# Order of the second running products, of the context state and of the second outputs in a linear-attention scan on one Trainium2 core

## Chip, cores and metric

One core of a Trainium2 chip. The metric is the device time of one execution in microseconds (us). TensorE is PE in the profile, VectorE is DVE, ScalarE is ACT, GpSimd is POOL and SyncE is SP; PEld is PE's weight load.

## What is computed

A block of a diffusion model on 2048 latent tokens and 256 context tokens, width 1024, in fp32: an adaptively scaled RMS norm, a gated linear recurrence (HGRN2) with 8 heads of 128 by 128 states in both directions, a readout, and a gated feed-forward network with a convolution. The change lies in the recurrence:

```python
def hgrn2_chunk_scan(q, k, v, logf, s0):
    """S_t = diag(f_t) S_{t-1} + k_t v_t^T, o_t = S_t^T q_t, in chunkwise form."""
    ...
    scores = jnp.einsum('bhnik,bhnjk->bhnij', qe, ke)
    scores = jnp.where(mask, scores, 0.0)
    o_intra = jnp.einsum('bhnij,bhnjv->bhniv', scores, v)
    kv = jnp.einsum('bhnjk,bhnjv->bhnkv', k * jnp.exp(b_last - b), v)
    ...
    o_inter = jnp.einsum('bhnik,bhnkv->bhniv', q * jnp.exp(b), s_start)
```

The context tokens are scanned first, from a zero state; their final state in each direction starts the scan of the latent tokens.

## The kernel before

The stage of the change is `mixer_scan`, from about 560 to 1200 us of the span. It runs over two groups of 8 token tiles (g = 0 and 1), and in each group over the 8 heads. A head of group 0 begins with the projections of the context's two gates (`ctx_gates`); each head has two units of four 128-token tiles. For each unit PE projects the two gates (lines 943 to 945, three fp32r matmuls for one fp32 product; forward and backward direction), ACT makes the decay factors of them (967, 969), and then come the unit's steps:

- `factors`: running products of the decay factors on DVE (`tensor_tensor_scan`, 987), the differences "ke" of these (1002, 1003), and small products for each segment on POOL (1009 to 1031), the last of them "sd" (1012).
- `suffix`: the second running products, from the other end (two scans, 1037). They write S over the first ones, so they wait for POOL, which reads these.
- `rest`: the products of queries and keys with those factors (1044, 1045, 1052, 1021).
- `scores`: transposes of the keys (1075, with a copy on ACT, 1077), 96 small score matmuls into "sc" (1119), a masked copy of both directions (`copy_predicated`, 1136) and the sum of the two, "at" (1137).
- `stepped(0)`: the key-value products of the first two tiles into the PSUM tile "kv" (1150), two state updates on DVE (1153), and a copy of the other direction's products on ACT (sk, 1158) that is stored.
- `second`: the outputs of the first two tiles, `outputs(0)` (1173 from the states, 1176 from "at"), and `stepped(1)`.
- `outputs(1)`: the outputs of the last two tiles.

For the context of a head: `keys` (a product on DVE, 1021), a function that transposes them (1075, 1077), and `state`, which multiplies them with the values (1094, into the same PSUM tile "kv"; there is one bank with this tag) and makes the starting states `Sf[h]` and `Sb[h]` of it (1096 on ACT, 1097 to 1100 on DVE).

The order of all this is written as a clock. `at(when, f)` puts a function on an agenda, and each step of a latent projection (three matmuls) advances the clock by one; a step of the context's projection advances it by half. A gate pair of a unit takes 16 steps, that of the context 8. So a head of group 0 takes 40 steps, of group 1 32, and the steps of one unit run among the projections of the next. The numbers in `after` count from the end of the unit's gates. The second unit of a head ends its gates 16 steps after the first, so that the first unit's `scores` (19) come 3 steps after that end, and the second unit's `suffix` (6) 6 steps after it.

The agenda gives only a priority. A planner that works at build time, with costs of its own for each instruction, lays each engine's queue: of the instructions that it expects to be ready it takes the one that was listed first, so one that isn't ready is overtaken. On the chip each engine then runs its queue in that order. `tc.issue_after(i)` adds to this that what is listed in its block stands behind `i` in the queue of `i`'s engine. `tied(f)` uses it: it puts `f` behind the latest state update of a `stepped(0)` (`made_last`).

Of the kernel before, what the change touches and what calls it, by code (L numbers as in the profile page):

```python
# [16 lines left out]
OP = mybir.AluOpType  # L17
# [28 lines left out]
def body(ctx, tc, a, out):  # L46
    nc = tc.nc
    pe, act, dve, pool, sp = nc.tensor, nc.scalar, nc.vector, nc.gpsimd, nc.sync
# [848 lines left out]
    def mixer_scan():  # L897
# [31 lines left out]
        AB = fix.tile([128, 2, UT, 128], F32, name="AB")  # L929
# [140 lines left out]
        def turned(kd, s0, n):  # L1070

            tr = ps.tile([128, n, 2, 128], F32, name="tr", tag="tr")
            for i in range(n):
                for d in range(2):
                    pe.transpose(tr[:, i, d], kd[:, d, 4 * (s0 + i):4 * (s0 + i) + 4], ident)
            kt = gp.tile([128, 2, 2, 128], F32, name="kt", tag="kt", bufs=2)
            act.activation(kt[:, 0:n], tr, AF.Copy)
            return kt
# [31 lines left out]
        def unit_steps(h, t0, m):  # L1110

            kts, states = [], []
            at_ = gp.tile([128, UT, 128], F32, name="at", tag="at", bufs=2)
            q_ = act if h == NH - 1 and t0 == NT - UT else sp

            def scores():

                def score(d, s, k, kc, q, qc):
                    pe.matmul(scs[d][32 * kc:32 * kc + 32, s, 32 * qc.start:32 * qc.stop], k, q,
                              start=True, stop=True, skip_group_check=True)  # L1120

                ke, qp, km = [m[n] for n in ("ke", "qp", "km")]
                kts.append(turned(m["kd"], 0, 2))
                for s in range(UT):
                    for j in range(4):
                        qc = slice(2 - j // 2 * 2, 4 - j // 2 * 2)
                        score(0, s, km[:, s, j], j,
                              qp[:, 1 - j // 2, 4 * s + qc.start:4 * s + qc.stop], qc)
                    for d in range(2):
                        for j in range(4):  # L1130
                            qc = slice(j // 2 * 2, j // 2 * 2 + 2) if j % 2 == 1 - d \
                                else slice(j, j + 1)
                            score(d, s, ke[:, d, 4 * s + j], j,
                                  qp[:, d, 4 * s + qc.start:4 * s + qc.stop], qc)
                kts.append(turned(m["kd"], 2, 2))
                dve.copy_predicated(AB, masks, sc2)
                dve.tensor_tensor(at_, AB[:, 0], AB[:, 1], OP.add)

            def stepped(p):

                if p == 0:
                    states.append(gp.tile([128, UT - 1, 128], F32, name="states", tag="states",
                                          bufs=1))
                kt, sd, qi, v = kts[p], m["sd"], m["qi"], m["v"]
                late = is_late(h, t0 + 2 * p + 1)
                st = [f_state(h, t0)] + [states[0][:, i] for i in range(UT - 1)] + [f_state(h, t0)]
                kv = ps.tile([128, 2, 2, 128], F32, name="kv", tag="kv")
                for d in (1, 0):
                    for i in range(2):
                        pe.matmul(kv[:, d, i], kt[:, i, d], v[:, 2 * p + i], start=True, stop=True)  # L1150
                for i in range(1 if late else 2):
                    s = 2 * p + i
                    moved = dve.scalar_tensor_tensor(st[s + 1], st[s], sd[:, 1, s:s + 1], kv[:, 1, i],  # L1153
                                                     OP.mult, OP.add).ins
                if p == 0:
                    made_last.append(moved)
                sk = gp.tile([128, 2, 128], F32, name="sk", tag="sk", bufs=2)
                act.activation(sk, kv[:, 0], AF.Copy)  # L1158
                if late:
                    last_kv.append(sk)  # L1160
                n, s = 1 if late else 2, 2 * p
                q_.dma_start(stashed(t0 + s, n, 0, h), sk[:, 0:n])
                sp.dma_start(stashed(t0 + s, n, 1, h), qi[:, 0, 4 * s:4 * (s + n)].rearrange(
                    "p (j g) t -> p j (g t)", g=4))

            def outputs(p):
                st = [f_state(h, t0)] + [states[0][:, i] for i in range(UT - 1)]
                o = ps.tile([128, 2, 128], F32, name="o", tag="o")
                qi, v = m["qi"], m["v"]
                for i in range(2):  # L1170
                    s = 2 * p + i
                    late = is_late(h, t0 + s)
                    pe.matmul(o[:, i], qi[:, 1, 4 * s:4 * s + 4], st[s], start=True, stop=False)
                    if late:
                        pe.matmul(o[:, i], qi[:, 0, 4 * s:4 * s + 4], Sb[:, h], start=False, stop=False)
                    pe.matmul(o[:, i], at_[:, s], v[:, s], start=False, stop=True)
                n = 1 if late else 2
                if late:
                    last_out(o[:, 1])
                so = gp.tile([128, 2, 128], F32, name="so", tag="so", bufs=2)  # L1180
                act.activation(so[:, 0:n], o[:, 0:n], AF.Copy)
                q_.dma_start(stashed(t0 + 2 * p, n, 2, h), so[:, 0:n])

            def second():
                outputs(0)
                stepped(1)

            return scores, lambda: stepped(0), second, lambda: outputs(1)

        def keep_gate(h, t0, g):  # L1190
# [4 lines left out]
                    (act if h == NH - 1 and t0 >= HT else sp).dma_start(  # L1195
                        stash[t0 + i][:, 3, h], g[:, i])

        made_last = []

        def tied(f):  # L1200
            with tc.issue_after(made_last[-1]):
                return f()

        spare = []
# [134 lines left out]
        def head(g, h):  # L1339
            t0 = [HT * g, HT * g + UT]  # L1340
            last = g == 1 and h == NH - 1

            def ctx_gates():
                for d in range(2):
                    gates(d, h, None, project(weight(g, h, 2 - d), None))
                cv = values(cv_d[h // 2][:, h % 2])
                kd, sd, keys = factors(h, None, None, None, None)
                for dt, f in zip((5, 9, 12), (keys, *context_state(h, kd, sd, cv))):
                    at(clock[0] + dt, f)

            def gate(u):
                for d in range(2):
                    gates(d, h, u, project(weight(g, h, 2 - d), u))

            def unit(u, after):
                n = t0[u] // UT
                q = gp.tile([128, UT, 128], F32, name="q", tag="q", bufs=1)
                sp.dma_start(q, q_d[h][n])
                m, suffix, rest = factors(h, u, t0[u], q, values(v_d[h][n]))
                behind = (lambda: tied(rest)) if made_last else rest  # L1360
                for f, dt in zip((suffix, behind, *unit_steps(h, t0[u], m)), after):
                    at(clock[0] + dt, f)

            def out_gate(hh, u):
                keep_gate(hh, t0[u], swish(project(weight(g, hh, 4), u), ("q", "kdc")[hh % 2 ^ u]))

            if g == 0:
                ctx_gates()
            gate(0)
            unit(0, (6, 11, 19, 21, 24, 27) if last else (6, 11, 19, 21, 26, 31))  # L1370
            n = order.index((g, h)) + 1
            ahead = [(*order[n], ty) for ty in (2, 1)] if n < len(order) else \
                [(g, hh, 4) for hh in (NH - 2, NH - 1)]
            for i, w in enumerate(ahead):
                at(clock[0] + 2 + 7 * i, lambda w=w: weight(*w))
            gate(1)
            unit(1, (5, 9, 17, 19, 21, 23) if last else (6, 11, 19, 21, 26, 31))
            if last:
                c = clock[0]
                for k in range(4):  # L1380
                    at(c + 2 + k, lambda k=k: load_out_weight(k))
                for n, k in enumerate((4, 5, 6, 7)):
                    at(c + 8 + n, lambda k=k: load_out_weight(k))
                out_gate(NH - 2, 1)
                out_gate(NH - 2, 0)
                out_gate(NH - 1, 0)
                for k in range(4):
                    at(clock[0] + 1 + 2 * k, lambda k=k: split_out_weight(k))
                out_gate(NH - 1, 1)
# [149 lines left out]
    begun, behind = [], []  # L1539
# [723 lines left out]
```

## Time and profile before

| what | us |
|---|---|
| median of three runs (2700.61 to 2706.9) | 2703.89 |
| the profiled execution, its own time | 2705.35 |
| its span in the profile | 2703.5 |
| PE busy | 2646.1 (98%) |
| DVE busy | 2074.4 (77%) |
| ACT busy | 1187.3 (44%) |
| POOL busy | 597.9 (22%) |

Rows of the profile have the form "line engine operation out<-in, shape, count". In a timeline the first two numbers are the start and the duration in us, and a bracket gives the idle time of the engine before the instruction and what ended it. In rows of stretches come the length and then, for each engine, the busy time and the count of instructions; after them the granted clock of PE (1.00 is full speed), the share of the DMA engines and GB/s. In rows of waits stand who waited, for whom, the total in us, how often, and the longest. Matmul rows start every 0.23 us for a 128x512 product although each is shown with 0.39 us, since matmuls overlap.

### The profile page before, as it was taken

To read this page: it belongs to the slowest core of one execution; us is meant where nothing else is said; L and a number is where in the kernel's file an instruction comes from. 1 tells how busy PE (TensorE), PEld (TensorE's weight loads), DVE (VectorE), ACT (ScalarE), POOL (GpSimd) and SP (SyncE) were. 2 spreads that over 40 slices of the span, in tenths; PEclk is the share of its full clock that TensorE was granted. 3 is DMA by queue.
4 is the path that set the end of the run, shared out by engine and by line. 5 is a ranking of instruction groups with operands and counts; after the bars stand their busy time and mean duration, and the time that the engine had idled before them with its cause. 6 is when DMAs were issued, how large, how long until landed. Compare 5 with 4: busy or idle time off the path is not lost.

```text
span 2703.5 us, 42065 instructions
## 1 busy us (share of the span) xinstructions
PE 2646.1 (98%) x15800; PEld 2205.9 (82%) x15800; DVE 2074.4 (77%) x2953; ACT 1187.3 (44%) x2051; POOL 597.9 (22%) x934
## 2 busy tenths in 40 slices
PE   7899999999999999999999999999999999999998
PEld 4787788888888888888887888888888888888887
DVE  4856766667887889878887878877887777578896
ACT  4645534433333233345566444443444444333444
POOL 1000222321222121111112444334433440000001
PEclk9999999999999999999999999999999999999999
DMA  8755655363445665548887322227232224888653
GB/s 341 276 198 195 233 197 183 102 248 120 151 152 175 217 204 180 163 138 310 294 315 278 107 81 94 86 71 296 94 94 68 86 81 159 301 283 285 206 180 133
DMA packets 257915, 498.12 MB, mean 184 GB/s; under 512 B 28192, under 2 KB 141232, under 8 KB 249136
## 3 DMA queue, kind: packets, MB, share of 16 engines
q1 hardware_dynamic: 252992, 486.20, 52.5%
q10 hardware_dynamic: 4720, 9.24, 0.9%
q8 instruction: 124, 2.03, 0.3%
q14 instruction: 79, 0.65, 0.1%
HBM read 335.70 MB, written 159.66 MB: 183 GB/s over the span
## 4 chain that ended last, share of the span: by engine, by line
PE 72%; DVE 10%; DMA 3%; POOL 1%; ACT 1%; issue 1%; SPq 0%; POOLq 0%; DVEq 0%; ACTq 0%
PE y L2076 4%; PE y L2075 4%; PE y L2077 4%; PE z L943 3%; PE z L945 3%; PE z L944 3%; PE zc L1474 3%; PE zc L1476 3%; PE zc L1477 3%; PE zd L1476 3%; PE za L1476 3%; PE za L1477 3%; PE zd L1477 3%; PE zd L1474 3%; PE za L1474 3%; PE y L1580 2%
## 5 line engine op out<-in xcount | busy, mean ns | idle before, releaser
L80 ACT ACTIVATE w<-raw 128x512 fp32r<-128x512 f32 (+1 forms) x286 | 186.1, 656 | 215.9 <-PE zd L1477 75.0
L81 DVE TENSOR_TENSOR w<-raw,w 128x512 fp32r<-128x512 f32 (+1 forms) x286 | 226.8, 797 | 64.3 <-ACT w L80 61.8
L81 DVE TENSOR_TENSOR w<-s,w 128x512 fp32r<-128x512 f32 x195 | 173.0, 892 | 81.8 <-ACT w L80 80.2
L2075 PE MATMUL y<-w,mh 128*128 128x512 f32 x600 | 233.4, 390 | 0.6 <-ACT X L2109 0.6
L2076 PE MATMUL y<-w,mh 128*128 128x512 f32 x600 | 233.5, 389 | 0.2 <-DVE w L81 0.2
L2077 PE MATMUL y<-w,ml 128*128 128x512 f32 x600 | 233.4, 389 | 0.0
L80 ACT ACTIVATE w<-s 128x512 fp32r<-128x512 f32 x195 | 121.7, 630 | 204.8 <-POOL s L220 82.5
L76 POOL TENSOR_TENSOR rs<-rs,mhalf 128x1 f32<-128x1 f32 (+3 forms) x53 | 58.2, 1102 | 446.5 <-DVE rs L75 433.9
L943 PE MATMUL z<-tok,w 128*128 128x512 f32 x352 | 145.6, 414 | 0.0
L1474 PE MATMUL zc<-rT,w 128*128 128x512 f32 x352 | 137.1, 389 | 1.9 <-DMA rT<-rhs1T 1.9
L945 PE MATMUL z<-tok,w 128*128 128x512 f32 x352 | 138.5, 394 | 0.0
L944 PE MATMUL z<-tok,w 128*128 128x512 f32 x352 | 138.0, 392 | 0.0
L1158 ACT ACTIVATE sk<-kv 128x256 f32<-128x256 f32 x64 | 24.6, 384 | 256.4 <-DVE states L1153 121.1
L1476 PE MATMUL zc<-rT,w 128*128 128x512 f32 x352 | 137.0, 389 | 0.0
L1477 PE MATMUL zc<-rT,w 128*128 128x512 f32 x352 | 136.9, 389 | 0.0
L219 POOL TENSOR_TENSOR s<-raw 128x512 f32<-128x512 f32 x54 | 90.6, 1677 | 194.9 <-DMA raw<-in_w_up_dram 128.7
L2075 PEld LDWEIGHTS y<-w,mh 128*128 128x128 f32 x600 | 112.6, 188 | 24.9 <-ACT X L2109 1.5
L2076 PEld LDWEIGHTS y<-w,mh 128*128 128x128 f32 x600 | 112.6, 188 | 23.8 <-DVE w L81 0.6
L2077 PEld LDWEIGHTS y<-w,ml 128*128 128x128 f32 x600 | 112.6, 188 | 23.6
L1476 PE MATMUL za<-rB,w 128*128 128x512 f32 x336 | 130.7, 389 | 0.0
L1477 PE MATMUL za<-rB,w 128*128 128x512 f32 x336 | 130.7, 389 | 0.0
L1474 PE MATMUL za<-rB,w 128*128 128x512 f32 x336 | 130.7, 389 | 0.0
(466 smaller groups left out, 7750.9 us busy)
## 6 DMA issues: line engine op xcount, KB each, us to landing
raw<-in_w_up_dram SPq DMA_DIRECT2D x88, 512.0 KB, 3.5
raw<-in_w_in_dram SPq DMA_DIRECT2D x75, 512.0 KB, 5.2
w<-w SPq DMA_DIRECT2D x32, 1024.0 KB, 6.1
lr<-m SPq DMA_DIRECT2D x49, 512.0 KB, 4.6
m<-r SPq DMA_DIRECT2D x66, 256.0 KB, 3.5
spare<-in_w_ada_dram SPq DMA_DIRECT2D x32, 512.0 KB, 5.1
kq<-stash SPq DMA_DIRECT2D x15, 1024.0 KB, 7.1
og<-stash SPq DMA_DIRECT2D x30, 512.0 KB, 5.1
```

Source lines behind the costliest of these rows:

```text
L80: i = act.activation(h, src, AF.Copy)
L81: j = dve.tensor_tensor(l, src, h.bitcast(F32), OP.subtract)
L219: eng.tensor_tensor(s1, a21, a22, OP.add)
L943: pe.matmul(z, w[:, 0, k], h, start=k == 0, stop=False, skip_group_check=True)
L944: pe.matmul(z, w[:, 0, k], l, start=False, stop=False, skip_group_check=True)
L945: pe.matmul(z, w[:, 1, k], h, start=False, stop=k == KT - 1, skip_group_check=True)
L1474: pe.matmul(o, w[:, 0, k], r[:, :, 0, k], start=start and k == 0, stop=False, skip_group_check=True)
L1476: pe.matmul(o, w[:, 0, k], r[:, :, 1, k], start=False, stop=False, skip_group_check=True)
L1477: i = pe.matmul(o, w[:, 1, k], r[:, :, 0, k], start=False, stop=k == 3, skip_group_check=True)
L2075: pe.matmul(z, lh, rh, start=start, stop=False, skip_group_check=True)
L2076: pe.matmul(z, lh, rl, start=False, stop=False, skip_group_check=True)
L2077: pe.matmul(z, ll, rh, start=False, stop=stop, skip_group_check=True)
```

## The change

Three things change.

1. Each sum of the scores (1137) is remembered in a list `summed`, and `suffix` of a unit is issued behind the latest sum, which is that of the unit ahead. `tied` gets the list as an argument, and looks at it when the step runs; with an empty list nothing is tied. So `rest` of the second unit of the first head, which was not tied before, now is.
2. The three steps of a head's context state come at 8, 15 and 21 steps after its gates in place of 5, 9 and 12.
3. In group 0 the first unit's `outputs(1)` come at 33 in place of 31.

```diff
                 dve.copy_predicated(AB, masks, sc2)
-                dve.tensor_tensor(at_, AB[:, 0], AB[:, 1], OP.add)
+                summed.append(dve.tensor_tensor(at_, AB[:, 0], AB[:, 1], OP.add).ins)
...
-        made_last = []
-
-        def tied(f):
-            with tc.issue_after(made_last[-1]):
+        made_last, summed = [], []
+
+        def tied(f, made=made_last):
+            with tc.issue_after(made[-1]) if made else ExitStack():
                 return f()
...
-                for dt, f in zip((5, 9, 12), (keys, *context_state(h, kd, sd, cv))):
+                for dt, f in zip((8, 15, 21), (keys, *context_state(h, kd, sd, cv))):
                     at(clock[0] + dt, f)
...
-                behind = (lambda: tied(rest)) if made_last else rest
-                for f, dt in zip((suffix, behind, *unit_steps(h, t0[u], m)), after):
+                steps = (lambda: tied(suffix, summed), lambda: tied(rest), *unit_steps(h, t0[u], m))
+                for f, dt in zip(steps, after):
                     at(clock[0] + dt, f)
...
-            unit(0, (6, 11, 19, 21, 24, 27) if last else (6, 11, 19, 21, 26, 31))
+            unit(0, (6, 11, 19, 21, 24, 27) if last else (6, 11, 19, 21, 26, 31 if g else 33))
```

No instruction is added or taken away.

## Prediction

> **What bounds the kernel now.** I read the engine totals first, then the stretches, then the waits of the scan, then the order of instructions at three places.
>
> ```profile
> span 2703.5 us, 42065 instructions
> PE 2646.1 (98%) x15800; PEld 2205.9 (82%) x15800; DVE 2074.4 (77%) x2953; ACT 1187.3 (44%) x2051; POOL 597.9 (22%) x934
> ```
>
> TensorE (PE) is busy 98% of the span, so a change that takes no matmul away can win only gaps of PE. The stretches place them (columns: busy time of PE, its weight loads, VectorE = DVE, ScalarE = ACT, GpSimd = POOL; granted clock; DMA):
>
> ```profile
> 600.00:605.00 5.00, 4.62 (x17) 3.96 (x18) 5.00 (x10) 1.47 (x4) 2.74 (x3) 0.66 0.53 157
> 692.00:735.00 43.00, 42.04 (x430) 36.74 (x431) 34.78 (x54) 14.87 (x28) 10.00 (x35) 1.00 0.42 139
> 1000.00:1100.00 100.00, 100.00 (x1095) 86.64 (x1095) 89.60 (x127) 29.68 (x58) 17.74 (x73) 1.00 0.59 193
> ```
>
> A head of group 0 (692 to 735) loses about 1 us of PE, group 1 (1000 to 1100) nothing; the first head has a stretch with the clock at 0.66. The waits of the scan, 575 to 1200 (total, times, longest), say for whom:
>
> ```profile
> ACT kt L1077 <- PE kv L1094: 20.4, 7, 2.9
> DVE S L1037 <- POOL sd L1012: 34.5, 32, 2.4
> PE o L1173 <- DVE states L1153: 4.4, 7, 0.8
> PEld kv L1150 <- ACT sk L1158: 3.8, 10, 0.8
> PE o L1176 <- DVE at L1137: 2.7, 3, 1.8
> ```
>
> The last three are what the change can win; the first two sit on engines with room.
>
> **The sum ahead of the second scans.** First head, DVE, then PE:
>
> ```profile
> 592.16 0.63 DVE L1003 TENSOR_TENSOR ke<-S 128x512 f32<-128x512 f32 x1
> 593.88 1.32 DVE L1037 TENSOR_TENSOR_SCAN S<-F,d 128x528 f32<-128x528 f32 x1 [1.10 <-POOL sd L1012]
> 595.13 1.28 DVE L1136 COPY_PREDICATED AB<-mbf,sc 128x1024 f32<-128x1024 uint32 x1
> 596.30 1.24 DVE L1037 TENSOR_TENSOR_SCAN S<-F,d 128x528 f32<-128x528 f32 x1
> 597.47 0.67 DVE L1137 TENSOR_TENSOR at<-AB 128x512 f32<-128x512 f32 x1
> ...
> 589.37 0.36 PE L1119 MATMUL sc<-qp,ke 128*32 128x32 f32 x16
> 596.02 0.38 PE L1173 MATMUL o<-Sf,qi 128*128 128x128 f32 x2
> 598.18 0.49 PE L1176 MATMUL o<-v,at 128*128 128x128 f32 x2 [1.79 <-DVE at L1137]
> 599.04 0.49 PE L1173 MATMUL o<-states,qi 128*128 128x128 f32 x2 [0.37 <-DVE states L1153]
> 599.37 0.39 PE L1176 MATMUL o<-v,at 128*128 128x128 f32 x2
> 600.38 1.48 PE L1150 MATMUL kv<-v,kt 128*128 128x128 f32 x8 [0.62 <-ACT sk L1158]
> 601.51 0.77 PE L943 MATMUL z<-rB,w 128*128 128x512 f32 x1
> 604.57 0.39 PE L944 MATMUL z<-rB,w 128*128 128x512 f32 x1
> ```
>
> The scores (L1119) end at 589.7, yet DVE waits 1.10 us for POOL, runs a scan, the masked copy, a second scan, and only then the sum. Tied behind the sum, both scans leave: copy at 592.8, sum from 594.0 to 594.7, then the two short state updates and the scans. PE needs the sum at 596.2, so it is 1.5 us early. What goes: 598.18 - 596.02 less the usual 0.22 of such a pair = 1.94; 599.04 - 598.18 less 0.33 = 0.53; 600.38 - 599.37 less 0.22 = 0.79. Then the clock: seven matmuls of 128x512 take 604.57 - 601.51 = 3.06 where the later ones step by 0.23, 1.61 in all: 1.45. First head: **4.7 us**.
>
> The scans add no work (two of 1.25) and now wait for copy and sum; behind them on DVE lie the products of the same unit (L1044 on), which were tied behind a state update already, and behind those the transposes of its keys. Without the second tie the products start no later: copy, sum, updates and two scans run without the POOL wait, because POOL ends within copy and sum. So DVE gains its 1.1 us here, and also in group 1:
>
> ```profile
> 923.77 0.63 DVE L1003 TENSOR_TENSOR ke<-S 128x512 f32<-128x512 f32 x1
> 925.50 2.47 DVE L1037 TENSOR_TENSOR_SCAN S<-F,d 128x528 f32<-128x528 f32 x2 [1.10 <-POOL sd L1012]
> 927.89 1.28 DVE L1136 COPY_PREDICATED AB<-mbf,sc 128x1024 f32<-128x1024 uint32 x1
> 924.10 0.36 PE L1119 MATMUL sc<-qp,ke 128*32 128x32 f32 x16
> ```
>
> The scores end at 924.46 and L1003 at 924.40: the copy starts at once. Cover is thin there, but DVE would wait 1.1 us anyway. If the planner puts the state updates ahead of the scans, DVE waits instead for the kv matmuls, which follow the scores by two steps, and the 1.1 us stay lost; no PE work is late in either order. The earlier updates free ACT's copy of kv (sk) and the bank for the next kv matmuls:
>
> ```profile
> 728.38 0.39 PE L1176 MATMUL o<-v,at 128*128 128x128 f32 x2
> 728.90 1.16 PE L1150 MATMUL kv<-v,kt 128*128 128x128 f32 x8
> ```
>
> 0.52 less 0.22 = 0.30 each, in 9 of the 10 waits counted above (the tenth is in the first head): **2.7 us**. The two later waits for the sum are 2.7 - 1.8 = 0.9 idle, with about 0.15 each of refill: **1.2 us**.
>
> **Second outputs 2 steps later.** Steady head of group 0, DVE and PE:
>
> ```profile
> 733.18 1.22 DVE L1021 TENSOR_TENSOR kd<-ke,TB 128x1024 f32<-128x1024 f32 x1
> 734.32 0.34 DVE L1153 SCALAR_TENSOR_TENSOR states<-states,sd,kv 128x128 f32<-128x128 f32 x1
> 733.34 0.38 PE L1173 MATMUL o<-states,qi 128*128 128x128 f32 x2
> 733.56 0.39 PE L1176 MATMUL o<-v,at 128*128 128x128 f32 x2
> 734.71 0.49 PE L1173 MATMUL o<-states,qi 128*128 128x128 f32 x2 [0.76 <-DVE states L1153]
> ```
>
> The outputs stand behind a state update that is queued after a 1.22 us product. The pair costs 1.15 - 0.22 = 0.93. The row of waits counts seven with 4.4 us: 0.37 is the first head's, and five such as this one at 0.76 make 3.8, which leaves a small one. A step is three matmuls of 0.23, 0.69; two steps are 1.38, more than 0.93, and DVE is some 0.8 us earlier besides: **4.6 us** gone. What moves along: four matmuls, a copy on ACT and one store on SP, whose data are read only after the scan; cost nothing while SP has nothing urgent there, at worst one copy ahead of a sigmoid on an ACT that is 44% busy. Gains so far 4.7 + 2.7 + 1.2 + 4.6 = **13.2 us**.
>
> **Context state later.** Per head of group 0 after the first (seven): a product on DVE, four transposes and a copy on ACT some steps later, then eight state matmuls (L1094), a copy and three small DVE operations, 9 steps later; no DMA, nothing on POOL. ACT's 2.9 us wait for L1094 goes, worth nothing by itself. The new place is 3 steps after the second kv product of the unit, and both write the one bank "kv" (below the first matmul after that product, then a scan, and the update and the copy that read the bank last):
>
> ```profile
> 706.69 0.48 PE L943 MATMUL z<-tok,w 128*128 128x512 f32 x1
> 708.71 1.32 DVE L1037 TENSOR_TENSOR_SCAN S<-F,d 128x528 f32<-128x528 f32 x1 [0.85 <-POOL sd L1012]
> 709.96 0.31 DVE L1153 SCALAR_TENSOR_TENSOR Sf<-states,sd,kv 128x128 f32<-128x128 f32 x1
> 710.37 0.38 ACT L1158 ACTIVATE sk<-kv 128x256 f32<-128x256 f32 x1 [3.91 <-DVE Sf L1153]
> ```
>
> The bank is read until 710.75. The step at 706.69 is the first of the three, of 0.69 each, so L1094 is due at 708.8: PE would stand 1.95 us if the planner issues L1094 there, 1.25 after one step more, 0.55 after two, nothing after three. How a planner that orders by its own costs errs is seen in the one present case of the same bank:
>
> ```profile
> 698.82 1.05 PE L1094 MATMUL kv<-v,kt 128*128 128x128 f32 x8
> 701.94 1.13 PE L1150 MATMUL kv<-v,kt 128*128 128x128 f32 x8
> ```
>
> L1150, one step behind in the list, was held back three steps and still came a little before the bank was free. So it does hold back, and somewhat too little; here the chain also holds a wait of 0.85 us for POOL: the planner put that scan ahead of the update, so it expected it ready at once. Ends: 0 and 1.95 a head; below 0 the 2.9 us of ACT give no PE time. I take one to two steps of holding back, 0.9 a head: 7 x 0.9 = **+6.3 us**, between the ends because the nearest row holds back and errs.
>
> **Sum.** -13.2 + 6.3 = -6.9. The profiled execution took 2705.35 us (span 2703.5), 1.46 above the median of the runs, 2703.89; against its own time 2698.4, against the median **2697.0**.
>
> **Clock.** 1.79 + 0.37 + 0.62 us of idle PE between 596.3 and 600.4 were followed by 3.4 us at half clock (0.66 over the five from 600 to 605 is 3.4 of 0.5), single stalls of 0.76 by none. [...]
>
> **Rivals.** (B, other side) The planner issues L1094 at once: seven stalls of 1.95 are 13.7, and if four of them fall whole into one window of the clock, 4 x 1.45 = 5.8 more: +19.5 - 13.2 = +6.3, 2710. For it: the planner underrates this chain; against: it held back three steps before. It decides from 1.9 us a head, clock included. (C) L1094 is held back past the bank's release, or the two updates go ahead of the scan: no loss, -13.2, 2690.7. (D) The change doesn't do all it says: in the new order the update before the second outputs moves back as far as the outputs, so 4.6 stays lost: -8.6 + 6.3 = -2.3, 2701.6.
>
> **Numbers.** Forecast (0.3 to 1.3 a head lost) 0.36, C 0.26, B 0.20, D 0.18. A measurement tells about 0.2%, 5.4 us. Faster: most of the forecast, 0.29, and C, 0.26: 0.55. Same: D, 0.17, the forecast's rest, 0.07, half of B's mild forms, 0.06: 0.30. Slower: rest of B and D, 0.15. Range 2689 to 2709: C's full gain, and B without a little of its clock; the forecast's own is 2694 to 2701.
>
> **What would show it.** L1137 directly after L1136, ahead of L1037; no row "o L1176 <- at" and no clock of 0.66 near 600; no waits of L1173 on states in group 0; L1094 in the seven heads with an idle gap ending on ACT sk or DVE Sf, its size the disputed number. Wrong if those gaps exceed 1.9 us, if the scan's gains come back as a wait later (the end of the scan near 1200), or if the new order on DVE delays the transposes of a unit's keys (L1075).

## The result

| | median, us | ratio to before, 95% interval |
|---|---|---|
| before (six runs, 2700.61 to 2706.9) | 2703.87 | |
| after (six runs, 2692.84 to 2695.72) | 2694.26 | 0.9964 [0.9955, 0.9974] |

The change makes the kernel 9.6 us faster, 0.36%; the forecast was 6.9 us, 2697.0, in a range of 2689 to 2709. The profiled execution has a span of 2692.3 us, 11.2 under that of before.

The scan is where it happens. The first matmul of the context's gates (L943) starts it and the first one of the readout (L1578) ends it; in the rows below (count; shortest, median and longest duration in ns; first and last start in us) these are the first starts. Before:

```profile
L943 PE MATMUL z<-cxt,w x128: 277/283/365, 556.2 to 853.8; 128*128 128x256 f32 x128
L1578 PE MATMUL y<-wo,gh x16: 388/389/397, 1203.6 to 1217.4; 128*128 128x512 f32 x16
```

After:

```profile
L943 PE MATMUL z<-cxt,w x128: 277/283/365, 554.2 to 845.1; 128*128 128x256 f32 x128
L1578 PE MATMUL y<-wo,gh x16: 388/389/397, 1190.5 to 1205.2; 128*128 128x512 f32 x16
```

The scan takes 647.4 us before and 636.3 after, 11.0 less when taken before rounding. The scan of after also starts 2.0 us sooner, by a part that the change doesn't touch, so single profiles differ by some us elsewhere, and below I compare the scan's length.

Stretches of after, chosen like those of before:

```profile
600.00:605.00 5.00, 5.00 (x97) 4.29 (x99) 4.26 (x7) 2.55 (x5) 2.25 (x5) 1.00 0.49 127
675.00:717.00 42.00, 41.08 (x430) 36.25 (x429) 34.51 (x53) 15.39 (x28) 10.13 (x31) 1.00 0.45 140
1000.00:1100.00 100.00, 100.00 (x1059) 86.73 (x1046) 89.94 (x130) 32.16 (x59) 23.35 (x72) 1.00 0.59 193
```

The half clock near 600 is gone (1.00 in place of 0.66). A head of group 0 (42.0 us from one head's first score matmul to the next head's, 42.6 before) still loses 0.92 us of PE, and the waits of PE in the scan say why. The first row is of before, and stands beside the three that the prediction shows; the others are of after:

```profile
PE o L1173 <- ACT oi L1272: 3.9, 2, 3.0
...
PE kv L1094 <- ACT sk L1158: 6.5, 7, 0.9
PE o L1173 <- ACT oi L1272: 2.9, 2, 2.4
PE o L1173 <- DVE states L1153: 0.6, 1, 0.6
PEld kv L1150 <- ACT sk L1158: 0.5, 2, 0.3
```

The wait for the sum (L1137) is gone, that for the state updates fell from 4.4 us in seven to one of 0.6, that of the kv products' weight loads for the copy sk from ten to two, and seven waits of the context's state matmuls (L1094) for the bank are new. DVE in a steady head of group 0:

```profile
673.48 1.31 DVE L1136 COPY_PREDICATED AB<-mbf,sc 128x1024 f32<-128x1024 uint32 x1
674.82 0.69 DVE L1137 TENSOR_TENSOR at<-AB 128x512 f32<-128x512 f32 x1
675.43 2.46 DVE L1037 TENSOR_TENSOR_SCAN S<-F,d 128x528 f32<-128x528 f32 x2
677.81 0.32 DVE L1153 SCALAR_TENSOR_TENSOR states<-Sf,sd,kv 128x128 f32<-128x128 f32 x1
...
683.30 0.34 DVE L1153 SCALAR_TENSOR_TENSOR states<-states,sd,kv 128x128 f32<-128x128 f32 x1
683.56 1.22 DVE L1021 TENSOR_TENSOR kd<-ke,TB 128x1024 f32<-128x1024 f32 x1
```

The sum follows the masked copy, and both scans follow the sum without a gap: of the 32 waits of these scans for POOL (34.5 us) one is left (1.1 us). The later state update (683.30) now stands ahead of the 1.22 us product that it stood behind before.

### The profile page after: what moved, and what is told of

Its sections match the earlier page's. It is cut to its first block, busy times and chain, and to the rows that moved or that the text cites. A ratio compares the mean times of both kernels' runs of the same rounds, so it can differ in the third digit from the quotient of the medians.

```text
span 2692.3 us, 42039 instructions
## 1 busy us (share of the span) xinstructions
PE 2639.1 (98%) x15800; PEld 2204.6 (82%) x15800; DVE 2076.6 (77%) x2953; ACT 1195.5 (44%) x2051; POOL 609.9 (23%) x934
## 3 DMA queue, kind: packets, MB, share of 16 engines
q8 instruction: 124, 2.03, 0.3%
## 4 chain that ended last, share of the span: by engine, by line
PE 79%; DVE 4%; DMA 2%; ACT 1%; issue 1%; POOL 1%; POOLq 0%; DVEq 0%; SPq 0%; ACTq 0%
PE z L943 4%; PE z L945 4%; PE z L944 4%; PE y L2077 4%; PE y L2076 4%; PE y L2075 4%; PE zc L1474 3%; PE zc L1476 3%; PE zc L1477 3%; PE zd L1474 3%; PE za L1476 3%; PE zd L1476 3%; PE zd L1477 3%; PE za L1477 3%; PE za L1474 3%; PE y L1578 2%
## 5 line engine op out<-in xcount | busy, mean ns | idle before, releaser
L943 PE MATMUL z<-tok,w 128*128 128x512 f32 x352 | 145.7, 414 | 0.0
L1474 PE MATMUL zc<-rT,w 128*128 128x512 f32 x352 | 137.0, 389 | 1.6 <-DMA rT<-rhs1T 1.6
L987 DVE TENSOR_TENSOR_SCAN S<-F,d 128x528 f32<-128x528 f32 (+1 forms) x80 | 91.4, 1142 | 54.9 <-ACT F L969 54.8
L1474 PE MATMUL za<-rB,w 128*128 128x512 f32 x336 | 130.7, 389 | 0.0
```

The source lines that it names most:

```text
L943: pe.matmul(z, w[:, 0, k], h, start=k == 0, stop=False, skip_group_check=True)
L987: dve.tensor_tensor_scan(flat(S[:, d]), flat(F[:, d]), flat(d1[:, 0:ns]), 0.0, OP.mult, OP.max)
L1474: pe.matmul(o, w[:, 0, k], r[:, :, 0, k], start=start and k == 0, stop=False, skip_group_check=True)
```

## Experiments

Two readings were open. One: the three parts add up, each with the terms of the forecast. The other: they depend on each other through the planner's order. All kernels below are timed beside runs of before on the same chip. The table gives the scan's length by the trace, cut at the first score matmul (L1119) of three units of group 0: the first unit of all, the first unit of head 1, and the first unit of head 7. So "heads 1 to 7" is six heads long. Differences in the text are taken before rounding.

| kernel | to first scores | first head | heads 1 to 7 | rest | scan | ratio to before |
|---|---|---|---|---|---|---|
| before | 32.2 | 46.3 | 254.7 | 314.2 | 647.4 | |
| after | 31.6 | 43.3 | 252.1 | 309.3 | 636.3 | 0.9964 [0.9955, 0.9974] |
| e1 tie alone | 31.6 | 43.5 | 248.7 | 309.3 | 633.1 | 0.9960 [0.9947, 0.9972] |
| e2 context alone | 31.6 | 47.0 | 260.4 | 312.8 | 651.8 | 1.0033 [1.0022, 1.0045] |
| e3 outputs alone | 32.5 | 46.2 | 254.4 | 312.7 | 645.7 | 1.0002 [0.9993, 1.0011] |
| e4 without context | 32.9 | 43.5 | 248.2 | 307.7 | 632.2 | 0.9953 [0.9941, 0.9966] |
| e5 context at 26 | 31.6 | 42.1 | 245.2 | 307.8 | 626.7 | 0.9923 [0.9910, 0.9935] |
| e6 behind updates | 31.6 | 42.2 | 252.1 | 306.1 | 632.0 | 0.9947 [0.9934, 0.9961] |
| e7 context at 18 | 31.6 | 42.6 | 252.1 | 307.8 | 634.1 | 2693.33 us, one run |
| e8 updates and 26 | 31.6 | 41.0 | 245.2 | 306.1 | 623.9 | 0.9919 [0.9905, 0.9932] |
| e9 tie and 26 | 31.6 | 42.2 | 245.2 | 307.8 | 626.8 | 0.9936 [0.9923, 0.9949] |
| e10 after again | 31.6 | 43.3 | 252.1 | 309.3 | 636.3 | 0.9963 [0.9949, 0.9977] |
| e11 without context again | 31.7 | 43.5 | 248.6 | 309.3 | 633.1 | 0.9949 [0.9936, 0.9961] |

Two rows of one kernel tell how far a column can be trusted: after and e10 agree, e4 and e11 differ by 1.2 us ahead of the first scores and by 1.6 in the rest. The 1.6 is a stretch of 3.41 us at half clock. Such a stretch lies in the first head of before, e2 and e3, and in the rest of before, after, e1, e10 and e11, and nowhere else in these scans.

**e1: part 1 of the change alone, the second scans behind the sum.** On the kernel after (lines cut at the dots):

```diff
-... zip((8, 15, 21), (keys, ...
+... zip((5, 9, 12), (keys, ...
...
-... (6, 11, 19, 21, 26, 31 if g else 33))
+... (6, 11, 19, 21, 26, 31))
```

> The kernel after with the context state back at 5, 9, 12 and the second outputs back at 31: only the second scans behind the sum are left. Theory A (the terms of the forecast add up): the first head's wait and its half clock go, and the waits for the copy of kv and for the sum, 8.6 us in all, 2695.3; the second outputs of group 0 still wait 0.76 us for the state update in five heads. Rival B (the three parts depend on each other): the tie already moves the state update ahead of the long product on VectorE, so the outputs' wait goes too, 13 us, 2691. Rival C: the tie is worth the first head alone, about 4 us, 2700.

Measured: 2693.39 us, 11.0 under before, about as much as the whole change brings; the scan is 14.2 us shorter than before, 3.2 shorter than after. PE's waits in the scan, and DVE in a steady head:

```profile
PE o L1173 <- ACT oi L1272: 2.9, 2, 2.4
PE tr L1075 <- DVE kd L1021: 1.8, 6, 0.7
PE o L1173 <- DVE states L1153: 0.8, 1, 0.8
...
686.89 0.34 DVE L1153 SCALAR_TENSOR_TENSOR states<-states,sd,kv 128x128 f32<-128x128 f32 x1
687.15 1.22 DVE L1021 TENSOR_TENSOR kd<-ke,TB 128x1024 f32<-128x1024 f32 x1
```

Rival B: the outputs of group 0 stand at 31 here, as before, and yet wait for no update, except once in the first head. The tie alone has moved the update ahead of the long product. A new wait has come, of the context's key transposes for their product: 0.72 us in the first head, and five of about 0.2.

**e2: the context state alone.** On the kernel before, (8, 15, 21) for (5, 9, 12).

> The kernel before with only the context state at 8, 15, 21. Theory A: the state matmuls wait for the bank of kv, 0.9 us of idle TensorE in each of seven heads, 6.3 us, less about 1 us of small waits that go: 2709. Rival B: the wait is paid back, because nothing of the context stands any more among the scores and the first kv products, and the planner no longer holds those back: 2704 or less, with the same seven waits in the trace.

Measured: 2712.4 us, 8.0 slower than the runs beside it (2704.36); the scan is 4.5 us longer. The seven new waits are there beside the old ones:

```profile
PE kv L1094 <- ACT sk L1158: 6.5, 7, 0.9
PE o L1173 <- DVE states L1153: 4.5, 7, 0.8
PE o L1176 <- DVE at L1137: 2.5, 3, 1.6
```

Theory A in its mechanism, though the time is 3.4 us above its 2709. Heads 1 to 7 take 5.7 us longer, 0.95 each, and the first head 0.7; the rest is 1.4 shorter, since it has no half clock here and that of before has one. Of what the time lost outside the scan, the profile shows 2.5 us behind the first matmul of the next stage (L1474), where a half clock from 1470.88 to 1474.29 follows a wait of 2.18 us for a DMA; before waits 1.89 there, without one.

**e3: the second outputs alone.** On the kernel before, 33 for 31 in group 0.

> The kernel before with only the second outputs of group 0 at 33. Theory A: the five waits of 0.76 us for the state update go, 0.93 us each with the refill, 4.6 us, 2699.3; the first head keeps its 1.79 us wait and the half clock. Rival B: the update stays as late as the outputs, since its place on VectorE is set by the planner's times, or the outputs now collide with the next transposes: 2704.

Measured: 2704.37 beside 2704.36, no change. The scan is 1.6 us shorter, as no half clock falls into its rest here, and the heads are as long as before. The updates no longer hold PE up, but something else does:

```profile
PE tr L1075 <- DVE kd L1021: 5.0, 7, 0.8
PE o L1176 <- DVE at L1137: 2.7, 3, 1.8
PE o L1173 <- DVE states L1153: 0.4, 1, 0.4
```

In a steady head, DVE and then PE:

```profile
734.72 0.69 DVE L1021 TENSOR_TENSOR kd<-ke,TB 128x512 f32<-128x512 f32 x1 [0.31 <-POOL TB L1015]
735.47 0.66 PE L1075 MATMUL tr<-ident,kd 128*128 128x128 f32 x4 [0.81 <-DVE kd L1021]
```

The outputs don't wait, and the context's transposes, which come right behind them, wait 0.81 us for a product (kd of 128x512) that stands some places behind the same long product (kd of 128x1024) on DVE. The wait moved from one user of the queue to the next; in the sense of its price, rival B.

**e4: the tie and the outputs, without the context.** On the kernel after, (5, 9, 12) again.

> The kernel after with only the context state back at 5, 9, 12. Theory A: the loss of the context state's new place, seven waits of 0.9 us, goes, and nothing else: 6.5 us under the kernel after, about 2688. Rival B: the new place pays for itself in another way (state matmuls out of the way of scores and kv products), so that the time is that of the kernel after within 2 us, or above it: 2693 to 2697.

Measured: 2693.01 us, 1.25 under the kernel after: rival B, by the time. The scan is 4.1 us shorter, of which 1.6 is a half clock that it doesn't have. The two kernels once more, beside each other:

> The kernel after once more, beside the next one on the same chip, to compare the two directly: 0.996 to 0.9965 of before. Theory A (the context's new place costs TensorE 4.1 us in the scan, as the two traces say): slower than the next kernel by 3 to 5 us. Rival B: the difference of the traces is lost elsewhere, and the two are equal within 1.5 us.

> The kernel after with only the context state back at 5, 9, 12, once more. Theory A: 3 to 5 us under the kernel after. Rival B: equal within 1.5 us.

Measured: after 2693.29, ratio 0.9963 [0.9949, 0.9977]; without the context 2691.16, ratio 0.9949 [0.9936, 0.9961]. The scans are 636.3 and 633.1 us. The medians differ by 2.1, the ratios by 0.0014, 3.8 us. Both pairs point the same way, but the intervals overlap, so the times alone don't show that the context's new place costs anything in the kernel after. It rests on the traces: heads 1 to 7 are 3.4 and 3.9 us longer there, the first head 0.2 shorter.

**e5: the context's state matmuls at 26.** On the kernel after, (8, 15, 26).

> The kernel after with the context's state matmuls at 26 in place of 21 (keys and transposes stay at 8 and 15). Theory A (the bank of kv is what they wait for): ScalarE's copy has then long read the bank, the seven waits of 0.92 us go with their refill, about 7 us in the scan: scan stage 629 us in place of 636.3, total near 2687. Rival B (TensorE is only let in later by a fixed chain, and the wait turns up again at the next user of the bank or of the keys): scan stage 634 to 637, total 2692 to 2695.

Measured: 2684.42 us, ratio 0.9923 [0.9910, 0.9935], about 10 us under the kernel after. PE's waits in the scan:

```profile
PE o L1173 <- ACT oi L1272: 2.9, 2, 2.4
PE o L1173 <- DVE states L1153: 0.6, 1, 0.6
```

Theory A: the seven waits are gone and no other took their place. Heads 1 to 7 take 245.2 in place of 252.1, 6.9 us for six waits, **1.15 each**: 0.92 of idle PE and 0.23 of refill, by which the first matmuls behind the wait start later still. The first head is 1.15 shorter too, so the waits of the kernel after cost it 8.0 us. The scan is 9.6 us shorter than after; the other 1.6 lie in the rest, and are the half clock (last section).

**e7: the context's state matmuls at 18.** On the kernel after, (8, 15, 18).

> The kernel after with the context's state matmuls at 18 in place of 21, which lists them at the second kv product itself. Theory A (the planner holds them back by the bank's release as it expects it, whatever the step): the same place in TensorE's queue, four steps behind the kv product, and the same seven waits of 0.92 us. Rival B (the step sets the place): they come 2 us sooner and wait 2.9 us each, 14 us in all, with a half clock behind some of them.

Measured: 2693.33 us in a single run; the scan is 2.2 us shorter than after, of which 1.6 is the half clock that its rest lacks. PE's waits:

```profile
PE kv L1094 <- ACT sk L1158: 6.5, 7, 0.9
PE o L1173 <- ACT oi L1272: 2.9, 2, 2.4
```

Theory A: listed three steps sooner, they take the same place in the seven heads and wait the same 0.92 us. So for these two steps the place isn't set by the list, but by the planner's idea of when the bank is free, and that is too early by those 0.92 us. The first matmul behind the kv product, the last one of the fourth step, and L1094, in the kernel after and then in e7:

```profile
697.83 0.48 PE L943 MATMUL z<-tok,w 128*128 128x512 f32 x1
700.45 0.39 PE L945 MATMUL z<-rB,w 128*128 128x512 f32 x1
701.76 1.16 PE L1094 MATMUL kv<-v,kt 128*128 128x128 f32 x8 [0.92 <-ACT sk L1158]
...
700.13 0.48 PE L943 MATMUL z<-tok,w 128*128 128x512 f32 x1
702.74 0.39 PE L945 MATMUL z<-rB,w 128*128 128x512 f32 x1
704.05 1.16 PE L1094 MATMUL kv<-v,kt 128*128 128x128 f32 x8 [0.92 <-ACT sk L1158]
```

**e6: second scans behind the latest state update.** On the kernel after (shortened):

```diff
+updated.append(moved)                 # each half's last update
-lambda: tied(suffix, summed)
+lambda: tied(suffix, updated)
```

> The kernel after with the second scans issued behind the latest state update (of either half of a unit) instead of behind the score sum. Theory A: in the first head the updates no longer stand behind two scans of 1.23 us, so the two waits of the kernel after near 594 us (0.75 and 0.31 us with refill) go; the context's waits stay, as the update that frees the bank stands behind a product and not behind a scan there: scan stage 635, total 2693. Rival B: the updates let the bank go earlier everywhere, the context's waits shrink to under 0.5 us: scan stage 631 or less. Rival C: VectorE now waits for the kv products before each second scan, its products come later, and TensorE waits for keys or outputs in group 1: scan stage above 637.

Measured: 2690.85 us, ratio 0.9947 [0.9934, 0.9961]; the scan is 4.3 us shorter than after. PE's waits, then DVE near the end of the scan, in after and in e6:

```profile
PE kv L1094 <- ACT sk L1158: 6.4, 7, 0.9
PE o L1173 <- ACT oi L1272: 1.5, 2, 1.0
...
1130.04 1.25 DVE L987 TENSOR_TENSOR_SCAN S<-F,d 128x528 f32<-128x528 f32 x1
1131.71 0.68 DVE L1270 TENSOR_TENSOR top<-top,oi 128x512 f32<-128x512 f32 x1
...
1133.72 0.68 DVE L1270 TENSOR_TENSOR top<-top,oi 128x512 f32<-128x512 f32 x1
1135.11 1.25 DVE L987 TENSOR_TENSOR_SCAN S<-F,d 128x528 f32<-128x528 f32 x1
```

Theory A for the first head (42.2 in place of 43.3) and for the context's waits, which stay. Not foreseen: the wait for ACT near the end of the scan shrinks from 2.4 to 1.0 us. There PE waits for ACT, and ACT for a sum on DVE (L1270); a first scan of 1.25 us (L987) stands ahead of that sum in after, and behind it in e6. No half clock follows the shorter wait; the two make the other 3.2 us. Nothing of rival C: PE has no new wait in group 1.

**e8: both edits**, and **e9: the tie and 26, with the outputs back at 31.**

> Both edits: second scans behind the latest state update, context's state matmuls at 26. Theory A: the two gains add, scan stage 628, total 2686, the fastest so far. Rival B: the order behind the updates costs what it wins, and the time is that of the kernel with 26 alone.

> The kernel after with the context's state matmuls at 26 and the second outputs of group 0 back at 31. Theory A (the two steps win nothing once the tie has moved the state update ahead of the long product): scan stage 627 us as with 33, total within 2 us of the kernel with 26 alone. Rival B: the outputs meet the update again, waits of 0.7 us in the heads of group 0, scan stage 630 to 632.

e8 has 2683.21 us, ratio 0.9919 [0.9905, 0.9932], scan 623.9: the gains add in the scan (2.7 us under e5), while the time lies within the interval of e5. In the profile the gain is lost right behind the scan: from the first L1578 to the first L1474 e8 takes 234.8 us and e5 232.0, and e8 has a half clock there (1197.42 to 1200.83) that e5 lacks. It has the lowest median here, 22.7 us under the runs of before beside it (2705.89). e9 has 2686.63 us, and the scan of e5 (626.8 to 626.7), with no wait of group 0's outputs behind the first head: theory A by the scan, the two steps win nothing once the tie is there. Its time is 2.2 us above e5's, just outside the 2 us that theory A allowed, but the intervals overlap.

## Why the prediction was right, and where it was not

- **The sum ahead of the scans: right in mechanism, and larger than its terms.** Forecast 8.6 us (4.7 + 2.7 + 1.2); e1 took 14.2 out of the scan and 11.0 out of the time. In the first head 4.7 was too much: the planner put the updates behind both scans, which the forecast had ahead of them, and 2.7 were won; two small waits stay (0.58 us at 594.65 in after, and a smaller one), which e6 takes away. The 2.7 for the copy of kv came much as forecast, with eight of ten waits gone. A steady head of group 0 won 1.1 us (42.6 to 41.5), mostly the wait of the second outputs, which the forecast had credited to the next part. Group 1 and the end of the scan won 5.0, of which about 2.4 were forecast; 1.0 of it is the wait for ACT (3.9 to 2.9 us), for which there was no term, and what is left of it stays open.
- **The second outputs 2 steps later: wrong.** The step gave them 4.6 us. They are worth nothing alone (e3) and nothing that the scan shows beside the tie (e9 against e5). The wait that they were to take away is in fact gone, through the tie: it moved the update ahead of the long product, while the prediction kept it behind. That the outputs' wait would only pass to the next in the queue was named by no rival; rival D had the update move back as well, and it moved forward.
- **The context state later: right, and the point on which the forecast turned.** It gave seven waits of 0.9 us of PE for the bank, with one to two steps of holding back; the trace has seven of 0.92 behind one held-back step, and e5 and e7 show that they are the bank's. Two sizes were off. The refill was left out: 1.15 us a wait, 8.0 in all for 6.3. And the later place was given no gain of its own, while it wins 0.65 us a head (41.53 in e1, 40.88 in e5), about 0.4 at the key transposes and 0.2 at the kv products. Net the part costs 0.5 us a head, and 3.2 in the scan (e1 and e11 against after).
- **Rival B** (waits of 1.95 us and half clocks) did not come: none of the 0.92 us waits is followed by a slow stretch. Its windows of the clock are shown by no row of the prediction; what the runs show of them are the steps of 3.41 us in the last section. **Rival C**, no loss at the bank, is what e5 has: the forecast gave 2690.7, and it has 2684.4, as the tie is worth more than its terms.
- **The sum.** 13.2 - 6.3 = 6.9 against 9.6 measured. The gain in the scan before the bank's loss is 11.0 + 8.0 = 19.0, not 13.2. That the forecast came so near is in part luck: the tie brought 5.6 us more than its terms, the outputs 4.6 less, the context cost 3.1 less, and of the 11.0 us some was lost again behind the scan. That loss is the prediction's own sign of being wrong, a gain that comes back as a wait near 1200, in a small form: the first product of the readout waits for ACT. Stretch of after, and the matmul:

```profile
1205.00:1215.00 10.00, 8.09 (x36) 6.44 (x35) 7.85 (x18) 3.43 (x6) 0.00 (x0) 0.83 0.98 400
1207.88 0.50 PE L1578 MATMUL y<-wo,ghl 128*128 128x512 f32 x1 [1.84 <-ACT ghl L80]
```

A wait of 1.84 us (1.39 before) and a half clock behind it. From the first L1578 to the first L1474, the next stage, before takes 231.6 us, after 234.4. The wait alone doesn't bring the half clock: e5 and e6 wait 1.74 and 1.73 us there and have none.

## What to carry to other kernels

Where an engine's order is laid by a planner, look at what stands ahead of the late instruction in its queue, not at the step that waits for it: giving the waiter two more steps only passed the wait on, and putting one short instruction ahead of two long ones took away three kinds of waits. Before work is moved to a new place, count the users of each single buffer around that place, with the time until the last reader is done; here five steps further made a loss of 8 us into none, while three steps nearer changed nothing. And try the parts of a change apart: this one held a part worth 11 us, one worth nothing, and one that cost 3 us of the scan.

## What was not expected of the hardware

The half clock is not a property of the kernel alone. In the scan and the readout it comes in stretches of 3.41 us, and their starts keep to a grid of that length: in before the two of the scan, at 601.07 and 1147.20, lie 82 and 242 such steps behind an earlier one at 321.18, and in e11 the one at 1132.90 lies 238 steps behind one at 320.52. e4 and e11 are the same kernel. Both have the same wait of PE, 4 us later in e4, and the same work on either side of it. Steps of the grid and the matmul that ends the wait, e4 (its grid counted on from its half clock at 322.05):

```profile
1131.01:1134.43 3.42, 2.83 (x13) 1.97 (x11) 3.42 (x8) 0.39 (x1) 0.52 (x2) 1.00 0.46 131
1134.43:1137.84 3.41, 1.64 (x11) 1.55 (x12) 1.55 (x5) 3.27 (x12) 1.02 (x1) 1.00 0.00 0
1137.84:1141.25 3.41, 3.41 (x109) 2.86 (x109) 1.87 (x5) 1.70 (x5) 2.12 (x10) 1.00 0.46 120
1136.20 0.49 PE L1173 MATMUL o<-states,qi 128*128 128x128 f32 x2 [2.37 <-ACT oi L1272]
```

and e11:

```profile
1129.49:1132.90 3.41, 1.04 (x8) 0.68 (x7) 2.19 (x7) 2.31 (x10) 0.81 (x3) 1.00 0.13 38
1132.90:1136.31 3.41, 3.41 (x12) 2.83 (x11) 2.17 (x4) 2.15 (x6) 2.02 (x8) 0.50 0.36 98
1132.22 0.49 PE L1173 MATMUL o<-states,qi 128*128 128x128 f32 x2 [2.37 <-ACT oi L1272]
```

In e11 the 2.37 us of idle PE lie whole within one step, and the next one runs at half clock; in e4 they are cut into 0.59 and 1.78 us, and PE runs on at full clock. The rest of the scan is 1.6 us longer in e11 (309.3 against 307.7). Eleven of the profiles have this wait with 2.4 to 3.0 us. Counted on the grid of each, where 2.03 us or more of idle PE fell into one step there, a half clock followed (before, after, e1, e10, e11); where the larger part was 1.78 us or less, none did (e2, e3, e4, e5, e7, e9). That is no threshold for other places: near 600 us, idle of 1.42 to 1.54 us in one step was enough in before, e2 and e3.

Gaps of 2.37 us (e11) and, in the readout of after, of 1.84 were followed by a half clock; the same 2.37 us in e4, and 1.74 and 1.73 in the readout of e5 and e6, were not. A wait of this length is worth its own time and, in some executions, about 1.6 us more.
